# Column tiles on x without scales in the opening of a hybrid attention layer

## The chip, the cores and the metric

The kernel runs on one core of a Trainium2 chip. The metric is the device time of one execution in microseconds (us). Engines: PE is TensorE (matrix products; PEld its weight loads), DVE is VectorE, ACT is ScalarE, POOL is GpSimd, and SP is the engine whose queue issues all loads and stores of this kernel. Each engine runs its instructions in the order in which they stand in its queue; one that waits holds up all behind it.

## The reference

One decoder layer over 2048 tokens with 1024 features, with 16 meta tokens ahead of them. What matters here is the head of it:

```python
def rms_norm(x, g):
    xf = x.astype(jnp.float32)
    y = xf * lax.rsqrt(jnp.mean(xf * xf, axis=-1, keepdims=True) + RMS_EPS)
    return (y * g.astype(jnp.float32)).astype(x.dtype)
...
    h = jnp.concatenate([pad, meta, x], axis=1)
...
        xn = rms_norm(h, norm_gain[l])
        proj = xn @ w_in[l]
        sb_q, sb_k, sb_v, sw_q, sw_k, sw_v, sb_z, sw_z, g_sb, g_sw = jnp.split(proj, offsets, axis=-1)
```

The columns of `proj` are the queries, keys and values of a stick-breaking attention (sb), those of a sliding-window attention (sw), and four gates. Both attentions, the gated branch projections, the output projection with the residual and a final norm follow. Each row of x has one scale (the rsqrt of its mean square) and each feature one gain, so `xn @ w` is also (x times gain) `@ w`, multiplied by the scale of its row afterwards.

## The kernel before

Tokens are cut into four groups of 512 (`GT`), features into eight blocks of 128 (`KT`). A **column tile** is 128 columns of `proj` for one group: its result stands transposed in one PSUM bank, columns on partitions and tokens along the bank. All products are made at nearly full precision from two parts: x and the weights are each split into a high part (rounded) and a low part (the difference), `xh`, `xl`, `wh`, `wl`. A column tile is then 8 blocks x 3 products = 24 products of 128x512 (`gemm`, L357 to L359). The tiles that also need the meta tokens append 16 small products to bank `zm` (L365).

The first two groups to run are 2 and 3 (`halves`). For each group the program

- loads x in rows, eight pieces of 128x512, squares them on ACT with a sum per row (L313), and works out the scale of each row (`scales`, `rsqrt`; L314, L117 to L124);
- spreads the scales over a bank with four transposes on TensorE (`spread`, L323) and copies them to `rb` (L335);
- loads x transposed (`xt`) in eight blocks, multiplies each by gain and `rb` on DVE (L341), casts to `xh` on ACT (L342) and takes `xl` on DVE, or on POOL for two blocks of the first group (L343).

A weight tile (`weights`) is a load of 512 KB (`raw`), a cast to `wh` (ACT at L106 in the opening, POOL at L108 later) and a difference `wl` (L109, on POOL in the opening, on DVE after it). Both halves are written to DRAM, for the second half of the program reads them again.

TensorE's instructions run in the order of the program text (`tc.manual_schedule`). For the other engines and for SP's queue a planner chooses the order. The opening is: scales of group 2 and of the meta tokens; `prep` of group 2; sb_k0 and sb_q0 on group 2, their products interleaved; scales and `prep` of group 3; sb_k1 on group 2; the same three tiles on group 3; then sw_k on both groups, sw_v on both groups, and the queries. What a tile does with its bank stands in its `use`: for sb_k and sb_q a high and a low part (L112, L113) written to DRAM; for sw_k the rotary embedding (L545 to L549) and four copies (L557, L559). Meta columns of sb_k are turned by a small transpose later (`meta_cols`, L377), in a function put on `pending`, which runs inside the next tile after its seventh block (`lagged`).

PSUM banks are rings by name: g and z and t have two, zm and o have one.

Of the kernel before, what the change touches and what calls it, by code (L numbers as in the profile page):

```python
# [16 lines left out]
P = 128  # L17
D = 1024
# [21 lines left out]
def f32(ap):  # L40
    return ap.bitcast(F32)
# [3 lines left out]
def tile_kernel(ctx, tc, x, xt, meta, metat, gain, w_in, w_sb, w_sw, w_out, sinks, fgain,  # L45
# [106 lines left out]
    wp = ctx.enter_context(tc.tile_pool(name="w", bufs=1, side="right"))  # L152

    kept = {}

    def weights(c0, w=w_in):
# [8 lines left out]
        raw = wp.tile([P, KT, P], F32, tag="raw", name="raw", bufs=2)[:, :n, :]  # L165
        DMA(raw, w[c0 // P])
        split(wh, wl, raw)
        kept[key] = [dram(f"{t}_{w.name}_{c0}", [P, n, P], F32R) for t in "hl"]
        for t, k in zip((wh, wl), kept[key]):
            DMA(k, t)  # L170
        return wh, wl


# [129 lines left out]
    def ring_x(dt=F32):  # L303
        return tp.tile([P, GT], dt, tag="xs", name="xs", bufs=XS)

    def scales(src, rows, n, mk=ring_x):

        ssq = tp.tile([P, 2, 4], F32, tag="ssq", name="ssq", bufs=2)
        for i in range(n):
            for f in range(2):  # L310
                t = mk()
                DMA(t[:rows], src[i * rows:(i + 1) * rows, f * GT:(f + 1) * GT])
                A.activation(t[:rows], t[:rows], AF.Square, accum_out=ssq[:rows, f, i:i + 1])  # L313
        V.tensor_tensor(ssq[:rows, 0, :n], ssq[:rows, 0, :n], ssq[:rows, 1, :n], op=ALU.add)  # L314
        rs = tp.tile([P, 4], F32, tag="rs", name="rs", bufs=2)
        rsqrt(rs[:rows, :n], ssq[:rows, 0, :n], tp)
        return rs
# [5 lines left out]
            T.transpose(acc[:, i * rows:(i + 1) * rows], rs[:rows, i:i + 1].to_broadcast([rows, P]), ident[:rows, :rows])  # L323
        return acc[:, :n * rows]

    def group_scales(g, mk=ring_x):
        return scales(x[g * GT:(g + 1) * GT, :], P, 4, mk)

    def prep(g, rs, mk=ring_x, pool=False, mid=lambda: None):

        xh[g] = xp.tile([P, KT, GT], F32R, tag=f"xh{g % 2}", name="xh")
        xl[g] = xp.tile([P, KT, GT], F32R, tag=f"xl{g % 2}", name="xl")
        rows = spread(rs, P, 4)
        rb = tp.tile([P, GT], F32, tag="rb", name="rb", bufs=1)
        A.copy(rb, rows)  # L335
        for k in range(KT):
            if k == MID:
                mid()
            t = mk()
            DMA(t, xt[g, k])  # L340
            V.scalar_tensor_tensor(t, t, gn[:, k:k + 1], rb, op0=ALU.mult, op1=ALU.mult)  # L341
            A.copy(xh[g][:, k, :], t)  # L342
            (G if pool and k in XP else V).tensor_tensor(xl[g][:, k, :], t, f32(xh[g][:, k, :]), op=ALU.subtract)  # L343

    def prep_meta(rs):
        t = ring_x()[:, :KT * NM].rearrange("p (k t) -> p k t", k=KT)
# [7 lines left out]
    def gemm(acc, w, g, pm=None):  # L354
        wh, wl = w
        for k in range(KT):
            T.matmul(acc, lhsT=wh[:, k, :], rhs=xh[g][:, k, :], start=k == 0, stop=False)  # L357
            T.matmul(acc, lhsT=wh[:, k, :], rhs=xl[g][:, k, :], start=False, stop=False)  # L358
            T.matmul(acc, lhsT=wl[:, k, :], rhs=xh[g][:, k, :], start=False, stop=k == KT - 1)  # L359
            if k < KT - 1 or pm is not None:  # L360
                yield 0.65
        if pm is not None:
            for k in range(KT):
                for t in (wh, wl):
                    T.matmul(pm[:48, :P], lhsT=mx[:, k, :], rhs=t[:, k, :], start=k == 0 and t is wh,  # L365
                             stop=k == KT - 1 and t is wl)

    def meta_sum(pm):

        t = tmp(rows=NM)[:, :P]  # L370
        A.copy(t, pm[32:48, :P])
        V.tensor_tensor(t, pm[0:NM, :P], t, op=ALU.add)
        return t

    def meta_cols(ms):
        tr = ps("zm")
        T.transpose(tr[:, :NM], ms, ident[:NM, :NM])  # L377
        return tr[:, :NM]

# [475 lines left out]
    hsplit[0] = False  # L855
    rs = group_scales(halves[0][1])
    for half, groups in enumerate(halves):
        with tc.tile_pool(name=f"swa{half}", bufs=1, side="left") as sp:
            m = half == 0
            vsplit[0] = True  # L860
            if not m:
                ts = [mk() for mk in sbt[:3]]
                rs = rs1
            if m:
                for _ in zip(*(by_group([t], groups[:1], m) for t in ts[:2])):
                    pass
                flush_all()
            else:
                drain(by_group(ts[:2], groups[:1], m))
            prep(groups[1], rs)  # L870
            drain(by_group(ts[2:], groups[:1], m), by_group(ts, groups[1:]))
# [12 lines left out]
            flush_all()  # L884
        with tc.tile_pool(name=f"sb{half}", bufs=1, side="left") as bp:
            vsplit[0] = False
            side = stick(groups, bp)
            drain(tiles_by_tile(gts[2:3], groups))
            if half == 0:
                rs0, rs1 = (group_scales(g) for g in halves[1])  # L890
            n_mid = 22 if half == 0 else 20
            cost_sb = 8 * sum(4 * (4 - g) for g in groups) * 1.31 + 16 * 0.75
            weave(tiles_by_tile(gts[3:3 + n_mid], groups), side, cost_sb / (n_mid * 10.4))
            drain(side)
        if half == 0:
            ts = [mk() for mk in gts[3 + n_mid:]]
            drain(by_group(ts, groups[:1]), by_group(ts[:1], groups[1:]))
            prep(halves[1][0], rs0)
            drain(by_group(ts[1:], groups[1:]))
        else:  # L900
            ringl = rings()
            osw = {}
            todo = [(k, g) for k in range(8) for g in halves[0]]
            for mk in gts[3 + n_mid:]:
                if mk is gts[-1]:
                    with tc.manual_schedule(engines={mybir.EngineType.Activation}):
                        drain(tiles_by_tile([mk], groups))
                        A.preload_act_table_set("natural_log_exp_and_others")
# [58 lines left out]
```

## Time and profile before

| | us |
|---|---|
| median of 3 runs | 2213.93 |
| lowest and highest | 2213.37, 2215.7 |
| profiled execution | 2219.62 |
| its span | 2217.9 |

The profile shows one execution. Its page gives for each engine the busy time, its share of the span and the number of instructions. The timeline has one row for each instruction or run of like ones: start and duration in us, engine, line, operation, output <- inputs, shape, and in brackets the idle time before it and what ended it. The view of windows has for each stretch its length, the busy time of PE, PEld, DVE, ACT and POOL with instruction counts, TensorE's granted clock, the DMA share and GB/s. TensorE's granted clock over the whole execution is 0.993 of full speed.

### The profile page before, as it was taken

Reading aid. Unit: us, or ns where it says so; the run is one execution under the profiler, and the core shown is the slowest. Engines: PE = TensorE matmul, PEld = TensorE weight load, DVE = VectorE, ACT = ScalarE, POOL = GpSimd, SP = SyncE. Lnnn points to the kernel's source line nnn. Section 1 sums busy time; section 2 is a strip of 40 time slices with the busy share of each in tenths; the row PEclk is TensorE's granted clock in tenths of the full one; section 3 lists DMA queues with packets and bytes.
Section 4 is the critical chain, followed back from the end, with each engine's and each line's share of the span. In section 5 each row is a group of like instructions: output and inputs, shape, how many; then the busy total and the mean of one; then the engine's idle time right before and its main releaser. Section 6 shows DMA issues by size and latency. Waiting matters only on the chain.

```text
span 2217.9 us, 30245 instructions
## 1 busy us (share of the span) xinstructions
PE 2158.9 (97%) x10614; PEld 1773.3 (80%) x10614; DVE 1352.5 (61%) x2105; ACT 1004.6 (45%) x2325; POOL 384.8 (17%) x495
## 2 busy tenths in 40 slices
PE   4999999999999999999999999999999999999998
PEld 3878887788888887788887888888888888787886
DVE  4568776455554433677666888777774436454453
ACT  5457777433333323577764555555553301221121
POOL 2123333323223201133220000000000232000000
PEclk9999999999999999999999999999999999999999
DMA  8645456855555465444436433324323986368522
GB/s 295 216 159 180 172 172 225 274 183 190 173 168 177 144 212 185 161 171 159 154 132 186 119 118 111 117 93 131 115 84 108 350 287 199 137 221 281 164 89 86
DMA packets 175385, 382.48 MB, mean 172 GB/s; under 512 B 22945, under 2 KB 41057, under 8 KB 175233
## 3 DMA queue, kind: packets, MB, share of 16 engines
q1 hardware_dynamic: 175232, 380.54, 50.9%
q8 instruction: 84, 1.38, 0.3%
q14 instruction: 69, 0.56, 0.1%
HBM read 231.04 MB, written 149.36 MB: 172 GB/s over the span
## 4 chain that ended last, share of the span: by engine, by line
PE 91%; DMA 3%; DVE 2%; issue 2%; ACT 1%; POOL 0%; SPq 0%; DVEq 0%; POOLq 0%; ACTq 0%
PE ps_g L357 16%; PE ps_g L358 15%; PE ps_g L359 15%; PE ps_o L808 6%; PE ps_z L760 6%; PE ps_t L782 5%; PE ps_o L669 3%; PE ps_z L623 3%; PE ps_g L212 1%; PE ps_g L213 1%; PE ps_g L211 1%; PE ps_z L212 1%; PE ps_z L211 1%; PE ps_z L213 1%; PE ps_t L212 1%
## 5 line engine op out<-in xcount | busy, mean ns | idle before, releaser
L357 PE MATMUL ps_g<-xh,wh 128*128 128x512 f32 x1600 | 663.5, 415 | 4.2 <-ACT xh L342 2.2
L358 PE MATMUL ps_g<-xl,wh 128*128 128x512 f32 x1600 | 632.5, 395 | 6.2 <-DVE xl L343 6.2
L359 PE MATMUL ps_g<-xh,wl 128*128 128x512 f32 x1600 | 632.2, 395 | 0.0
L771 DVE TENSOR_TENSOR_SCAN row<-row 128x512 f32<-128x512 f32 (+2 forms) x320 | 367.8, 1152 | 198.7 <-POOL row L769 122.4
L359 PEld LDWEIGHTS ps_g<-xh,wl 128*128 128x128 f32 x1600 | 303.0, 189 | 68.0
L357 PEld LDWEIGHTS ps_g<-xh,wh 128*128 128x128 f32 x1600 | 304.4, 190 | 54.2 <-DVE tmp L547 2.8
L358 PEld LDWEIGHTS ps_g<-xl,wh 128*128 128x128 f32 x1600 | 304.4, 190 | 52.3 <-DVE xl L343 7.3
L764 ACT ACTIVATE row<-ps_z 128x512 f32<-128x512 f32 (+1 forms) x320 | 172.1, 538 | 285.1 <-PE ps_z L760 236.5
L113 DVE SCALAR_TENSOR_TENSOR wtl<-ps_t,wth 128x512 fp32r<-128x512 f32 (+1 forms) x320 | 190.4, 595 | 45.8 <-ACT wth L112 44.3
L112 ACT ACTIVATE wth<-ps_t 128x512 fp32r<-128x512 f32 (+1 forms) x320 | 170.4, 532 | 101.1 <-PE ps_t L782 96.3
L760 PE MATMUL ps_z<-kt,q 128*128 128x512 f32 (+3 forms) x640 | 185.1, 369 | 0.3 <-ACT row L764 0.3
L782 PE MATMUL ps_t<-ident,row 128*128 128x128 f32 x1088 | 171.6, 273 | 1.2 <-DVE row L771 1.2
L782 PEld LDWEIGHTS ps_t<-ident,row 128*128 128x128 f32 x1088 | 136.0, 140 | 37.8 <-DVE row L771 1.7
L769 POOL TENSOR_SCALAR_AFFINE_SELECT row<-row 128x128 f32<-128x128 f32 x128 | 42.8, 335 | 621.4 <-ACT row L764 563.6
L108 POOL TENSOR_SCALAR wh<-raw 128x1024 fp32r<-128x1024 f32 (+1 forms) x71 | 74.2, 1045 | 426.0 <-PE ps_g L358 267.7
L760 PEld LDWEIGHTS ps_z<-kt,q 128*128 128x128 f32 x640 | 118.9, 188 | 26.4 <-ACT row L764 0.8
L808 PE MATMUL ps_o<-wth,vc 128*128 128x512 f32 (+1 forms) x320 | 125.1, 391 | 0.2
L631 ACT ACTIVATE sc<-sc,nm 128x129 f32<-128x129 f32 x256 | 100.1, 394 | 38.0 <-DVE nm L629 37.4
L808 PE MATMUL ps_o<-wtl,vc 128*128 128x512 f32 (+1 forms) x320 | 116.8, 365 | 0.0
L499 ACT ACTIVATE tmp<-ps_g 128x512 f32<-128x512 f32 x112 | 67.1, 599 | 100.7 <-PE ps_g L359 94.2
L109 POOL TENSOR_TENSOR wl<-raw,wh 128x1024 fp32r<-128x1024 f32 (+1 forms) x45 | 102.9, 2287 | 18.7 <-ACT wh L106 15.6
L250 ACT CAST ringl<-gt 128x512 fp32r<-128x512 f32 x32 | 19.9, 622 | 127.0 <-DVE gt L248 120.3
(222 smaller groups left out, 3337.2 us busy)
## 6 DMA issues: line engine op xcount, KB each, us to landing
raw<-in_w_in SPq DMA_DIRECT2D x58, 512.0 KB, 5.1
h_in_w_in<-wh SPq DMA_DIRECT2D x58, 512.0 KB, 3.1
l_in_w_in<-wl SPq DMA_DIRECT2D x58, 512.0 KB, 3.1
wh<-h_in_w_in SPq DMA_DIRECT2D x58, 512.0 KB, 3.7
wl<-l_in_w_in SPq DMA_DIRECT2D x58, 512.0 KB, 4.8
q<-qd SPq DMA_DIRECT2D x128, 128.0 KB, 3.9
vc<-vd SPq DMA_DIRECT2D x48, 256.0 KB, 2.9
qd<-tmp SPq DMA_DIRECT2D x32, 256.0 KB, 2.4
```

The lines of the kernel that those rows point to most:

```text
L109: (V if vsplit[0] else G).tensor_tensor(l, src, f32(h), op=ALU.subtract)
L112: A.activation(h, acc, AF.Copy, scale=scale)
L113: V.scalar_tensor_tensor(l, acc, scale, f32(h), op0=ALU.mult, op1=ALU.subtract)
L357: T.matmul(acc, lhsT=wh[:, k, :], rhs=xh[g][:, k, :], start=k == 0, stop=False)
L358: T.matmul(acc, lhsT=wh[:, k, :], rhs=xl[g][:, k, :], start=False, stop=False)
L359: T.matmul(acc, lhsT=wl[:, k, :], rhs=xh[g][:, k, :], start=False, stop=k == KT - 1)
L631: A.activation(sc[:, hh, :], sc[:, hh, :], AF.Exp, bias=nm[:, hh:hh + 1], accum_out=den[:, hh:hh + 1])
L760: T.matmul(z[:, :w], lhsT=lq, rhs=kt[h][:, k0:k0 + w], start=t == 0, stop=t == 1)
L764: A.activation(r[:, :w], z[:, :w], AF.Sigmoid, scale=-1.0)
L771: V.tensor_tensor_scan(r[:, :w], r[:, :w], r[:, :w], last[j] if n else 1.0, op0=ALU.mult, op1=ALU.min)
L782: T.transpose(tr[:, j * P:(j + 1) * P], rows_of[h, g, n - (j > i), j][:, k0:k0 + P], ident)
L808: T.matmul(o[:, :n], lhsT=v, rhs=r, start=first and r is wh, stop=last and r is wl)
```

## The change

The opening (the "start" pool and what follows up to the windows) is written anew, with DVE, ACT and SP in the order of the program text too.

- The three tiles sb_k0, sb_q0 and sb_k1 of groups 2 and 3 run on x times gain without scales (`unscaled`: high part on ACT, low part on DVE, no `rb`). Their six banks (g, g, z; z, o, t) are multiplied by `rb` afterwards (`out_of`), and the result goes to the tile's `use`.
- The normalised x of both groups, which sw_k and all later tiles use, is made afterwards: for group 2 in place from the blocks loaded at first (`raws`), for group 3 from a second load of its blocks.
- x for the scales comes as whole blocks of 128x1024 (`wide`; one of group 2's four as two halves) and is squared ahead of use.
- Meta products are separated from the tiles (`gemm_meta`, `meta_product`).
- The first three weight tiles take `wl` on DVE (`vsplit`), and the stores of weight halves are put off (`put_off`). The weights of sw_k and sw_v are loaded in the opening (`raw2`, `ready`).
- Pairs or threes of `normal` go in turns (`in_turns`), so that DVE and ACT alternate between blocks.
- sw_k and sw_v then run by group: both on 2, then both on 3. The meta columns of sb_k1 go to a t bank instead of zm.

```diff
+    put_off, ready = [], {}
...
+    def weights(c0, w=w_in, raw=None):
+
+        if c0 in ready:
+            return ready.pop(c0)
...
-            DMA(k, t)
+            if put_off is None:
+                DMA(k, t)
+            else:
+                put_off.append((k, t))
...
+    def normal(g, k, t, rb):
+        V.scalar_tensor_tensor(t, t, gn[:, k:k + 1], rb, op0=ALU.mult, op1=ALU.mult)
+        A.copy(xh[g][:, k, :], t)
+        yield
+        V.tensor_tensor(xl[g][:, k, :], t, f32(xh[g][:, k, :]), op=ALU.subtract)
...
-                    mc = meta_cols(ms)
+                    mc = meta_cols(ms, "zm" if p != 1 else "t")
...
-    with tc.tile_pool(name="start", bufs=1, side="left") as bp:
-        mk = lambda: bp.tile([P, GT], F32, tag="x0", name="x0", bufs=17)
-        rs = group_scales(halves[0][0], mk)
-        rsm = scales(meta, NM, 1)
-        ts = [sbt[0]()]
-        prep(halves[0][0], rs, mk, True, lambda: ts.append(sbt[2]()))
-    prep_meta(rsm)
-    hsplit[0] = HS
-    ts.append(sbt[1]())
-    hsplit[0] = False
-    rs = group_scales(halves[0][1])
+    g0, g1 = halves[0]
+    with (tc.tile_pool(name="start", bufs=1, side="left") as bp,
+          tc.manual_schedule(engines={mybir.EngineType.DVE, mybir.EngineType.Activation, mybir.EngineType.SP})):
+        hsplit[0] = vsplit[0] = True
...
+        def unscaled(g, k, t):
+
+            DMA(t, xt[g, k])
+            uh, ul = xh["u", g][:, k, :], xl["u", g][:, k, :]
+            A.activation(uh, t, AF.Copy, scale=gn[:, k:k + 1])
+            V.scalar_tensor_tensor(ul, t, gn[:, k:k + 1], f32(uh), op0=ALU.mult, op1=ALU.subtract)
...
+        def out_of(g, n, rb):
+            t = tmp()
+            V.tensor_tensor(t, accs[g, n], rb, op=ALU.mult)
+            yield
+            ts[n][1](g, t, ms[n] if g == g0 else None)
...
+        ts = [sbt[0]()]
+        x_tiles(("u", g0), 1)
+        for k in range(KT):
+            raws.append(bp.tile([P, GT], F32, tag="raw0", name="raw0", bufs=KT))
+            unscaled(g0, k, raws[k])
+        ts.extend([sbt[2](), sbt[1]()])
+        rsm = scales(squares(meta, NM, 1), NM, 1)
+        products(g0, 0, "g")
+        products(g0, 1, "g")
+        prep_meta(rsm)
...
+        rows = [wide(g0, i) for i in range(3)]
+        for i, t in enumerate(rows):
+            square(t, ssq0, i)
...
+        rs = scales(ssq0, P, 4)
+        products(g0, 2, "z")
...
+        for k in range(KT):
+            if k == 2:
+                rb0 = scale_rows(rs, bp.tile([P, GT], F32, tag="rb0", name="rb0"))
+            unscaled(g1, k, bp.tile([P, GT], F32, tag="raw1", name="raw1", bufs=4))
+        products(g1, 0, "z")
+        x_tiles(g0, 0)
+        rows = [wide(g1, i) for i in range(3)]
+        raw2 = [load(c) for c in (C_SWK, C_SWV)]
...
+        for k in range(0, KT, 2):
+            in_turns(*(normal(g0, j, raws[j], rb0) for j in (k, k + 1)))
+            if k == 2:
+                meta_product(0)
+            if k:
+                square(rows[k // 2 - 1], ssq1, k // 2 - 1)
+        t = wide(g1, 3)
...
+        square(t, ssq1, 3)
+        products(g1, 1, "o")
+        meta_product(2)
+        hsplit[0] = False
+        ready.update({c: weights(c, raw=raw) for c, raw in zip((C_SWK, C_SWV), raw2)})
+        new = [ring_x() for _ in range(4)]
+        for k, t in enumerate(new):
+            DMA(t, xt[g1, k])
+        in_turns(*(out_of(g0, n, rb0) for n in range(2)))
+        rs = scales(ssq1, P, 4)
+        products(g1, 2, "t")
+        rb1 = scale_rows(rs)
+        for k, t in put_off:
+            DMA(k, t)
+        x_tiles(g1, 1)
+        in_turns(out_of(g0, 2, rb0), normal(g1, 0, new[0], rb1))
+        for k in range(1, KT):
+            if k >= 4:
+                new.append(ring_x())
+                DMA(new[k], xt[g1, k])
+        in_turns(*(normal(g1, j, new[j], rb1) for j in (1, 2)))
+        in_turns(*(normal(g1, j, new[j], rb1) for j in (3, 4)))
+        in_turns(*(normal(g1, j, new[j], rb1) for j in (5, 6, 7)))
+    put_off = None
+    for n in range(3):
+        drain(out_of(g1, n, rb1))
...
-            drain(tiles_by_tile([sw_k, sw_v], groups, m), tiles_by_tile(q[0], groups[:1]), tiles_by_tile(sbt[3:4], groups, m))
+            if m:
+                drain(by_group([sw_k(), sw_v()], groups, m))
+            else:
+                drain(tiles_by_tile([sw_k, sw_v], groups))
+            drain(tiles_by_tile(q[0], groups[:1]), tiles_by_tile(sbt[3:4], groups, m))
```

More of the change, by code (lines that the diff above doesn't have):

```diff
@@ L154, in tile_kernel, with load @@
     kept = {}
-    def weights(c0, w=w_in):
+    put_off, ready = [], {}
+    def load(c0, w=w_in):
+        raw = wp.tile([P, KT, P], F32, tag="raw", name="raw", bufs=2)[:, :w.shape[2], :]
+        DMA(raw, w[c0 // P])
+        return raw
+    def weights(c0, w=w_in, raw=None):
+        if c0 in ready:
+            return ready.pop(c0)
         n = w.shape[2]
@@ L164, in weights @@
             return wh, wl
-        raw = wp.tile([P, KT, P], F32, tag="raw", name="raw", bufs=2)[:, :n, :]
-        DMA(raw, w[c0 // P])
+        raw = load(c0, w) if raw is None else raw
         split(wh, wl, raw)
@@ L324, in spread, with group_scales, scale_rows, x_tiles @@
         return acc[:, :n * rows]
[L326 to L335, printed above, removed]
+    def group_scales(g):
+        return scales(squares(x[g * GT:(g + 1) * GT, :], P, 4), P, 4)
+    def scale_rows(rs, rb=None):
+        if rb is None:
+            rb = tp.tile([P, GT], F32, tag="rb", name="rb", bufs=1)
+        A.copy(rb, spread(rs, P, 4))
+        return rb
+    def x_tiles(key, n):
+        xh[key] = xp.tile([P, KT, GT], F32R, tag=f"xh{n}", name="xh")
+        xl[key] = xp.tile([P, KT, GT], F32R, tag=f"xl{n}", name="xl")
+    def normal(g, k, t, rb):
[3 more added lines that the diff above has]
+        V.tensor_tensor(xl[g][:, k, :], t, f32(xh[g][:, k, :]), op=ALU.subtract)
+    def prep(g, rs):
+        x_tiles(g, g % 2)
+        rb = scale_rows(rs)
         for k in range(KT):
-            if k == MID:
-                mid()
-            t = mk()
+            t = ring_x()
             DMA(t, xt[g, k])
-            V.scalar_tensor_tensor(t, t, gn[:, k:k + 1], rb, op0=ALU.mult, op1=ALU.mult)
-            A.copy(xh[g][:, k, :], t)
-            (G if pool and k in XP else V).tensor_tensor(xl[g][:, k, :], t, f32(xh[g][:, k, :]), op=ALU.subtract)
+            drain(normal(g, k, t, rb))
     def prep_meta(rs):
@@ L362, in gemm, with gemm_meta @@
         if pm is not None:
[L363 to L366, printed above, removed]
+            gemm_meta(pm, w)
+    def gemm_meta(pm, w):
+        for k in range(KT):
+            for t in w:
+                T.matmul(pm[:48, :P], lhsT=mx[:, k, :], rhs=t[:, k, :], start=k == 0 and t is w[0],
+                         stop=k == KT - 1 and t is w[1])
     def meta_sum(pm):
-        t = tmp(rows=NM)[:, :P]
+        t = tp.tile([NM, P], F32, tag="ms", name="ms", bufs=2)
         A.copy(t, pm[32:48, :P])
@@ L863, in tile_kernel @@
                 rs = rs1
[L864 to L871, printed above, removed]
+            if not m:
+                drain(by_group(ts[:2], groups[:1]))
+                prep(groups[1], rs)
+                drain(by_group(ts[2:], groups[:1]), by_group(ts, groups[1:]))
             if m:
```

48 lines of the change are left out of this document (43 added, 5 removed).

## Prediction

> **What bounds the kernel now.** I read the page first, then TensorE's waits in the first 160 us, then the timeline there.
>
> ```profile
> span 2217.9 us, 30245 instructions
> PE 2158.9 (97%) x10614; PEld 1773.3 (80%) x10614; DVE 1352.5 (61%) x2105; ACT 1004.6 (45%) x2325; POOL 384.8 (17%) x495
> ...
> PE ps_t L323 <- DVE nwt L123: 17.8, 1, 17.8
> PE ps_t L323 <- DVE rs L124: 5.8, 1, 5.8
> PE ps_g L358 <- DVE xl L343: 3.9, 1, 3.9
> ```
>
> TensorE is busy for 97% of the span, and most of what is left is in the opening: 17.8 us until the scales of the first group (2) exist, 3.9 for its first low part, 5.8 for the scales of group 3 (target, releaser, us in total, times, longest). Everything behind the opening moves with it, so the question is at what time TensorE has the column tiles of the opening behind it.
>
> ```profile
> 21.04 0.79 PE L357 MATMUL ps_g<-xh,wh 128*128 128x512 f32 x1 [1.93 <-ACT xh L342]
> 25.71 0.79 PE L358 MATMUL ps_g<-xl,wh 128*128 128x512 f32 x1 [3.87 <-DVE xl L343]
> ...
> 39.18 0.22 PE L365 MATMUL ps_zm<-wh,mx 128*48 128x128 f32 x1
> ...
> 46.99 1.11 PE L323 MATMUL ps_t<-ident,rs 128*128 128x128 f32 x4 [5.80 <-DVE rs L124]
> 47.75 0.78 PE L357 MATMUL ps_g<-xh,wh 128*128 128x512 f32 x1
> 48.33 0.63 PE L358 MATMUL ps_g<-xl,wh 128*128 128x512 f32 x1
> 48.75 0.63 PE L359 MATMUL ps_g<-xh,wl 128*128 128x512 f32 x1
> ...
> 55.41 0.96 PE ps_zm L365 x16
> ...
> 72.80 0.39 PE L359 MATMUL ps_g<-xh,wl 128*128 128x512 f32 x1
> 73.02 0.39 PE L357 MATMUL ps_g<-xh,wh 128*128 128x512 f32 x1
> ...
> 97.98 0.59 ACT L416 COPY tmp<-ps_g 128x512 f32<-128x512 f32 x1 [0.16 <-PE ps_g L359]
> ```
>
> Starts 0.22 to 0.23 us apart are TensorE's full pace (72.80, 73.02), 0.43 its pace after a long wait (48.33, 48.75). A column tile of 24 products is thus 5.46 us. Six tiles (sb_k0, sb_q0, sb_k1 for two groups) come first, then sw_k and sw_v. The first product of sw_k stands at 73.02, and the last of sw_v at 97.9, where ACT reads its bank. These are my two marks. Work ahead of 73.0 is only 6 x 5.46 + 2 meta products at 0.96 (row x16, from the chain of waits): 35 us, so 38 us are lost.
>
> **The change part by part.** I carry the clock forward by the rows.
>
> *Tiles of group 2 without scales.* x-transposed and weights are loaded first; only gain is multiplied in, so the scales leave the front of the path.
>
> ```profile
> 1.70 3.90 SPq L55 DMA_DIRECT2D x<-in_x  x8
> 4.75 0.63 ACT L313 ACTIVATE x<-x 128x512 f32<-128x512 f32 x1 [2.69 <-DMA x<-in_x]
> 8.63 0.63 ACT L313 ACTIVATE x<-x 128x512 f32<-128x512 f32 x1 [0.51 <-DMA x<-in_x]
> 5.00:10.00 5.00, 0.00 (x0) 0.00 (x0) 0.00 (x0) 3.29 (x10) 0.00 (x0) 1.00 0.94 333
> 10.00:15.00 5.00, 0.00 (x0) 0.00 (x0) 0.79 (x5) 4.71 (x16) 0.22 (x1) 1.00 1.02 368
> 20.00:25.00 5.00, 0.79 (x1) 0.29 (x1) 5.00 (x6) 2.80 (x5) 2.63 (x1) 1.00 1.05 407
> 13.67 1.03 ACT L106 CAST wh<-raw 128x1024 fp32r<-128x1024 f32 x1
> 14.78 2.34 POOL L109 TENSOR_TENSOR wl<-raw,wh 128x1024 fp32r<-128x1024 f32 x1 [11.74 <-ACT wh L106]
> 14.83 2.30 DVE L121 TENSOR_TENSOR nwt<-rs 128x4 f32<-128x4 f32 x1 [0.81 <-ACT rs L119]
> 63.54 1.22 DVE L109 TENSOR_TENSOR wl<-raw,wh 128x1024 fp32r<-128x1024 f32 x1
> ```
>
> SP needs 0.49 us for an issue (3.90 for 8), so weights and eight blocks are issued by 6.1; the x loads for the squares, whole blocks now, are queued behind them. The first load of 256 KB landed at 4.75, the fourth at 8.63; later ones follow at 333 to 368 GB/s, at most 407 (last number of the window rows). The first weight block (512 KB) lands near 6, its cast takes 1.03 and its low part, now on DVE, 1.22 instead of 2.34 on POOL: ready at 8.2, with the first block of x (7.4 + two operations of about 0.65 = 8.7). Product 24 needs the eighth block, about 2.7 MB into the stream: 13 us. Some 11 products run at 0.43 until 13.5, 13 at 0.23: tile one ends at 16.2, tile two (sb_q0) at **21.7**. Before, tiles one and two, interleaved, ended at 39.2 (first meta product of L365).
>
> *Squares behind the meta tokens.* ACT's hand-made order has the copy of mx, which waits for a transpose behind tile two, ahead of the squares of x. So these begin at 22.7: three of 128x1024, at 1.03 for such a cast plus the read-out, about 1.2 each, and two of 128x512 at 0.8: 27.9. Group 2's scales then take what the chain below took.
>
> ```profile
> 45.24 0.16 DVE L314 TENSOR_TENSOR ssq<-ssq 128x4 f32<-128x4 f32 x1 [3.22 <-ACT xs L313]
> 48.14 0.59 ACT L335 COPY rb<-ps_t 128x512 f32<-128x512 f32 x1 [2.00 <-PE ps_t L323]
> 48.76 2.08 DVE L341 SCALAR_TENSOR_TENSOR xs<-xs,gn,rb 128x512 f32<-128x512 f32 x3 [1.83 <-ACT rb L335]
> 52.02 1.89 DVE L343 TENSOR_TENSOR xl<-xs,xh 128x512 fp32r<-128x512 f32 x3
> raw<-in_w_in SPq DMA_DIRECT2D x5, 512.0 KB, 5.9
> kd<-tmp SPq DMA_DIRECT2D x4, 256.0 KB, 2.0
> ```
>
> From L314 at 45.24 to the transposes at 46.99 is 1.75 us: 29.7. TensorE has meanwhile ended tile three at 27.5.
>
> *Group 3 without scales.* It has four buffers for eight blocks: loads five to eight each wait on SP until DVE is done with a block. Their landing is bounded by 2.0 (kd, empty queue) and 5.9 (raw, full queue); I take 2.5, since nothing else is in flight there. DVE starts at 29.7 and loses 1.2 to the copy of rb0, which ACT can do only after the transposes; so blocks three and four leave their buffers at 32.6 and 33.2, the last load lands at 35.7 and its two operations end at 36.9 (36.4 and 40.3 by the bounds). TensorE ends tile four at **37.6**; the last three products are all that is left then. Tiles five and six and two meta products (2 x 5.46 + 2 x 0.96) follow without a new wait: **50.4**.
>
> *DVE is the engine that is late next.* The edit gives it 16 unscaled low parts (0.65 each), 6 products with rb (0.66), 3 weight splits (1.22): 18 us more, and prep's 16 pairs stay. From 36.9: eight pairs of group 2 at 0.69 + 0.63 (rows x3: 2.08 and 1.89 by three) are 10.5, to 47.5; the sum of the second meta product waits for ACT's last square, 49.6; two weight splits 2.4; two products and two low parts 2.5; group 3's scales 1.75: 56.3. One thing adds to this: the high halves of the sw_k and sw_v weights stay on POOL and fall beside these DVE operations.
>
> ```profile
> 85.40 1.05 POOL L108 TENSOR_SCALAR wh<-raw 128x1024 fp32r<-128x1024 f32 x1 [0.47 <-POOL tmp L549]
> 85.47 1.00 DVE L548 TENSOR_TENSOR tmp<-tmp,sm 128x16 f32<-128x16 f32 x1
> ```
>
> A DVE operation on 16 columns took 1.00 beside such a POOL split, as the one on 4 took 2.30 above. The two splits cost DVE 0 to 2.1; I take 1, because DVE waits for ACT there anyway: **57.2**. The Trainium skill (SBUF — State Buffer, "SBUF: two separate sides") says that DVE and GpSimd lock one port pair for a whole instruction when the DVE operation has two SBUF inputs. These two rows agree with it (1.00 beside 1.05); by that rule all 2.1 would be paid and the sum below would be 1 us longer.
>
> *The mark.* The scale transposes of group 3 stand in TensorE's order ahead of sw_k. TensorE waits from 50.4 to 57.2 and starts sw_k at 58.0 (46.99 to 47.75 in the rows), against 73.0: 15.0 earlier. After so long a wait ten products run at 0.43 again: 2.1 back, so 12.9.
>
> *What is left to wait for.* From 57.2 DVE has the rest of its hand-made order: one product and its low part, eight pairs for group 3 (10.5), with about 2 of waits for ACT and for the last four loads behind four ring buffers: until 71.7. Behind it come three products with rb1, which release banks z, o and t, and the two small L399 parts. TensorE, in sw_k's first tile after its seventh block (64.6), transposes the two meta columns, the second into a t bank that the third product frees; and sw_k's own meta product goes into zm, which L399 reads. If DVE fits these four small operations into its gaps, TensorE runs on until sw_k of group 3 (73) needs x that is ready at 72 to 74. The low bound of these waits is 0, the high one 11.6 (second rival); I take 3.5, because DVE has two such gaps, and because of this:
>
> ```profile
> L187 ACT CAST ringl<-tmp x16: 620/622/629, 1718.1 to 1759.7; 128x512 fp32r<-128x512 f32 x16
> L908 ACT ACT_TABLE_LOAD  x1: 1283/1283/1283, 1755.5 to 1755.5; - x1
> ```
>
> L908 is in a hand-ordered part of ACT; casts of L187, outside it and emitted before it, ran until 1759.7. So operations outside a hand-ordered part do mix with it.
>
> *At no cost:* 2.1 MB of group 3 read twice and ten kept weight halves written later. They lie under TensorE's 13 us of tiles five and six and DVE's chain; without that cover the second reading costs 5 us at 407 GB/s. Of SP's issues in the two groups 32 loads of x become 33.
>
> **Sum:** 15.0 - 2.1 - 3.5 = 9.4 us, taken as 9 of the profiled span of 2217.9 (2219.6 with what lies around it). That execution stands 5.7 above the median of 2213.9; from the median, **2205**.
>
> **Rivals.**
>
> *Nothing waits behind the mark:* 12.9 us, **2201**. For it: x of group 3 is ready block by block. Against: DVE is the busiest engine there.
>
> *The banks are held to the end of DVE's order.* Then TensorE stands from 65.5 until the third product at 73.6, again from 74.4 to 75.9 for L399, and runs slow once more: 11.6 us. Gain 1.3: **2213**. For it: program order. Against: the L187 rows. This is also the case in which the change does not do what it says, TensorE being no earlier.
>
> *Slower: loads behind few buffers.* If the two sets of four loads land as in a full queue (5.9 less 2.5, of which 0.5 hides: 2.9 each), DVE's order ends at 77.5 instead of 71.7, and with the banks held 5.8 - 1.3 = 4.5 us are lost: **2218**. It decides from 73.0 on for the end of DVE's order. For it: writes of the kept weights are queued ahead of the second set. Against: those 2 MB have 6 us to drain.
>
> **How the numbers follow.** The forecast has 0.52, the first rival 0.16, the second 0.16, the third 0.16. A measurement here tells 0.2% (4.4 us) from no change. Faster by more: the first two cases, 0.68; within: 0.16; slower: 0.16. The forecast's own range is 2201 to 2209 (0 to 8 us of left waits); for 8 in 10 I go down to 2199, as the marks are good to 2 us, and up to 2217, short of the last rival.
>
> **What would show it.** TensorE's first product near 8 and not 21; the wait for group 3's scales near 50 to 57 as its longest; sw_k's first product at 58 (55 to 61); DVE without gaps from 30 to 57 but for the waits named; in sw_k's first tile no wait over 4 us on a bank read by DVE; ACT's read of the last sw_v bank at 88 or 89 instead of 97.9. Wrong would be a sw_k start after 66, or a wait of 8 us behind it.

## The result, and the profile after

| | before | after |
|---|---|---|
| median (9 runs each), us | 2215.58 | 2221.02 |
| lowest and highest | 2213.37, 2217.69 | 2216.67, 2224.83 |
| profiled execution, its span | 2219.62, 2217.9 | 2224.83, 2223.1 |
| ratio after to before, 95% interval | | 1.0028 [1.0019, 1.0037] |

The change makes the kernel 0.28% slower: 5.4 us more, where 2205 (10.6 less than this median of before) was forecast, with a range that ended at 2217. In the changed kernel `gemm` is L382 to L384, the meta products L393, the meta transposes L405, the copies of meta columns L426 (ACT) and L427 (DVE), `spread` L339, the rope L573 to L577, `out_of` L907. TensorE's waits of the first 160 us (target, releaser, us in total, times, longest):

```profile
PE ps_zm L393 <- DVE tmp L427: 11.2, 1, 11.2
PE ps_t L339 <- DVE rs L124: 7.9, 2, 6.3
PE ps_g L382 <- ACT xh L884: 7.4, 1, 7.4
PE ps_zm L393 <- DVE tmp L575: 3.3, 1, 3.3
```

The long waits of before (17.8 and 3.9 for group 2) are gone. Two new ones stand on bank zm, both at a meta product. The timeline of TensorE has the start of sw_k and both waits:

```profile
57.96 1.11 PE L339 MATMUL ps_t<-ident,rs 128*128 128x128 f32 x4 [6.31 <-DVE rs L124]
58.72 0.77 PE L382 MATMUL ps_g<-xh,wh 128*128 128x512 f32 x1
...
65.82 0.23 PE L405 MATMUL ps_zm<-ident,ms 16*128 16x16 f32 x1
...
78.25 0.34 PE L393 MATMUL ps_zm<-wh,mx 128*48 128x128 f32 x1 [11.24 <-DVE tmp L427]
...
91.19 0.34 PE L393 MATMUL ps_zm<-wh,mx 128*48 128x128 f32 x1 [3.35 <-DVE tmp L575]
```

sw_k starts at 58.72 instead of 73.02, **14.3 us earlier**. What follows takes it all back. The prediction's second mark was ACT's read of the last sw_v bank: 97.98 before, 88 or 89 forecast, 107.43 measured. ACT comes to that bank late in the changed kernel, behind four copies for sw_k, so the next bank is the better end of sw_k and sw_v: ACT's first read of a bank of the queries, in the timelines of before and of after.

```profile
103.92 0.59 ACT L545 ACTIVATE tmp<-ps_g 32x512 f32<-32x512 f32 x1 [0.16 <-PE ps_g L359]
```

```profile
104.87 2.54 ACT L585 CAST kk<-tmp 64x512 fp32r<-64x512 f32 x4 [2.78 <-POOL tmp L577]
107.43 0.59 ACT L444 COPY tmp<-ps_g 128x512 f32<-128x512 f32 x1
...
111.05 0.59 ACT L573 ACTIVATE tmp<-ps_g 32x512 f32<-32x512 f32 x1
```

This first read of a query bank is called **the mark** from here on. From the start of sw_k to it, it is 52.3 us after and 30.9 before, 21.4 more: 14.6 in the two waits (11.24 + 3.35), and the other 6.8 at a lower pace. The windows say where (length, then busy time and instructions of PE, PEld, DVE, ACT, POOL, then TensorE's granted clock, DMA share, GB/s), first before, then after:

```profile
58.00:80.00 22.00, 22.00 (x110) 18.00 (x109) 8.53 (x14) 3.22 (x8) 3.16 (x3) 1.00 0.81 288
80.00:100.00 20.00, 20.00 (x102) 16.35 (x101) 14.42 (x24) 13.33 (x29) 5.22 (x5) 1.00 0.38 127
100.00:2300.00 2200.00, 2088.96 (x10285) 1716.72 (x10283) 1300.13 (x2014) 958.47 (x2220) 362.26 (x470) 0.99 0.48 162
```

```profile
25.00:35.00 10.00, 7.82 (x32) 4.73 (x30) 5.24 (x12) 7.51 (x16) 0.00 (x0) 1.00 0.40 117
35.00:52.00 17.00, 15.76 (x88) 11.88 (x86) 14.27 (x21) 10.30 (x19) 2.10 (x2) 1.00 1.00 352
52.00:58.00 6.00, 0.04 (x1) 0.05 (x1) 5.20 (x13) 1.64 (x4) 0.00 (x0) 0.87 1.01 388
58.00:80.00 22.00, 10.76 (x47) 8.56 (x47) 14.76 (x24) 6.95 (x13) 3.14 (x5) 0.66 1.04 396
80.00:100.00 20.00, 16.66 (x74) 13.33 (x73) 9.92 (x22) 9.89 (x25) 2.38 (x3) 0.82 0.09 26
100.00:2300.00 2200.00, 2095.03 (x10317) 1721.34 (x10315) 1308.22 (x2022) 963.31 (x2229) 366.23 (x473) 1.00 0.48 163
```

Between 58 and 80 TensorE does 47 instructions where it did 110, at a clock of 0.66. Behind 100 us 10317 are left against 10285: 32 more, at 5.46/24 us each 7.3, which is the 7.1 by which the mark is later. The span grew by 5.2. The DMA engines are full from 35 to 80 after they had stood at 0.40 from 25 to 35.

What TensorE waits for 11 us is a copy of 128x16. The timelines of ACT and DVE show how it comes to be so late:

```profile
61.98 0.62 ACT L112 ACTIVATE tmp<-tmp 128x512 fp32r<-128x512 f32 x1
...
69.02 0.63 ACT L112 ACTIVATE tmp<-tmp 128x512 fp32r<-128x512 f32 x1 [0.65 <-DVE tmp L907]
75.38 0.63 ACT L112 ACTIVATE tmp<-tmp 128x512 fp32r<-128x512 f32 x1 [5.74 <-DMA kd<-tmp]
76.82 0.17 ACT L426 CAST tmp<-ps_zm 128x16 fp32r<-128x16 f32 x1 [0.80 <-DVE tmp L113]
```

```profile
76.05 0.69 DVE L113 SCALAR_TENSOR_TENSOR tmp<-tmp 128x512 fp32r<-128x512 f32 x1 [4.95 <-ACT tmp L112]
...
78.02 0.17 DVE L427 TENSOR_TENSOR tmp<-ps_zm,tmp 128x16 fp32r<-128x16 f32 x1
```

The meta transpose filled zm at 65.8 (L405 above). Its copy L426 stands in ACT's queue behind the high parts (L112) of group 3's three tiles. The last of these needs a free `tmp` tile, of which there are seven. By the order of the program one of them held the product that this step reads, and the other six held parts whose stores had not landed. ACT stands for 5.74 us; behind it come the low part L113 on DVE, L426, L427, and then TensorE. In the stretch 52 to 80 the stores took this long (queue's issues: count, KB each, median us to landing):

```profile
kd<-tmp SPq DMA_DIRECT2D x8, 256.0 KB, 6.6
h_in_w_in<-wh SPq DMA_DIRECT2D x3, 512.0 KB, 6.1
```

Before, four such stores of `kd` took 2.0 up to 60 us (their row stands in the prediction), and four more took 4.8 between 60 and 75. So the chain has four links: full DMA engines, seven `tmp` tiles, the place of the small copies in the queues, and one bank zm for both the transposes and the meta products. The experiments cut these links, alone and together.

A fifth link stands in SP's queue, and no run here cut it alone. The store that ACT waited for is, by the order of the program, the first of these two:

```profile
67.88 1.95 SPq L55 DMA_DIRECT2D kd<-tmp  x2
```

Its part was written by 62.6 (L112 at 61.98), and the low part that is stored with it by 63.3. SP issued the store only at 67.88, behind stores of weights and the loads of `ct` and `sn`, and it then took 7.4 us to land. So some 5 of its 12.8 us passed in SP's queue.

### The profile page after: what moved, and what is told of

It reads as the page before. It is cut to its first block, busy times and chain, and to the rows that moved or that the text cites. A ratio compares the mean times of both kernels' runs of the same rounds, so it can differ in the third digit from the quotient of the medians.

```text
span 2223.1 us, 30264 instructions
## 1 busy us (share of the span) xinstructions
PE 2163.1 (97%) x10614; PEld 1773.3 (80%) x10614; DVE 1369.6 (62%) x2134; ACT 1013.7 (46%) x2327; POOL 376.3 (17%) x490
## 5 line engine op out<-in xcount | busy, mean ns | idle before, releaser
L382 PE MATMUL ps_g<-xh,wh 128*128 128x512 f32 x1568 | 650.8, 415 | 9.7 <-ACT xh L884 7.4
L383 PE MATMUL ps_g<-xl,wh 128*128 128x512 f32 x1568 | 619.9, 395 | 3.6 <-DVE xl L359 3.0
L384 PE MATMUL ps_g<-xh,wl 128*128 128x512 f32 x1568 | 619.1, 395 | 0.0
L384 PEld LDWEIGHTS ps_g<-xh,wl 128*128 128x128 f32 x1568 | 296.8, 189 | 66.5
L382 PEld LDWEIGHTS ps_g<-xh,wh 128*128 128x128 f32 x1568 | 298.4, 190 | 58.4 <-ACT xh L884 7.4
L383 PEld LDWEIGHTS ps_g<-xl,wh 128*128 128x128 f32 x1568 | 298.4, 190 | 48.8 <-DVE xl L359 4.0
L113 DVE SCALAR_TENSOR_TENSOR wtl<-ps_t,wth 128x512 fp32r<-128x512 f32 (+1 forms) x320 | 190.3, 595 | 45.0 <-ACT wth L112 43.5
L112 ACT ACTIVATE wth<-ps_t 128x512 fp32r<-128x512 f32 (+1 forms) x320 | 170.4, 532 | 101.0 <-PE ps_t L810 96.3
L109 POOL TENSOR_TENSOR wl<-raw,wh 128x1024 fp32r<-128x1024 f32 (+1 forms) x42 | 94.8, 2257 | 3.2
```

Of the source, the lines that this page charges most:

```text
L109: (V if vsplit[0] else G).tensor_tensor(l, src, f32(h), op=ALU.subtract)
L112: A.activation(h, acc, AF.Copy, scale=scale)
L113: V.scalar_tensor_tensor(l, acc, scale, f32(h), op0=ALU.mult, op1=ALU.subtract)
```

## The experiments

All start from the changed kernel; line numbers behind an edit shift by up to four. "Left" is the number of TensorE instructions behind 100 us in the profiled execution; "mark" is the mark above. Both are of one execution each: group 3's scales came at 57.96 in the changed kernel and at 59.33 and 59.15 in e2 and e3, which are alike up to there, so marks are good to some 1.5 us. Theory T blames the full DMA engines and late stores, theory Z the bank zm and the order by hand, whatever the bytes; in the later runs O is the place in the queues and the order of DVE's and ACT's work, S the slots and stores.

| run | edit | median (runs) | ratio to before, 95% | mark | left |
|---|---|---|---|---|---|
| changed kernel | | 2221.02 (9) | 1.0028 [1.0019, 1.0037] | 111.05 | 10317 |
| e1 | kept weight halves stored earlier | 2221.09 (9) | 1.0023 [1.0013, 1.0033] | 112.70 | 10326 |
| e4 | four blocks of x not loaded twice | 2222.79 (7) | 1.0026 [1.0015, 1.0036] | 110.19 | 10313 |
| e2 | three more tiles | 2214.02 (11) | 0.9996 [0.9987, 1.0005] | 103.80 | 10285 |
| e3 | meta products in bank z | 2214.19 (12) | 0.9995 [0.9986, 1.0005] | 103.46 | 10283 |
| m5 | small copies placed by hand | 2215.70 (12) | 1.0001 [0.9993, 1.0009] | 105.18 | 10291 |
| m6 | e3, e4 and m5 | 2214.06 (11) | 0.9992 [0.9983, 1.0001] | 102.13 | 10278 |
| m7 | no order by hand | 2218.02 (10) | 1.0009 [0.9999, 1.0018] | 106.77 | 10298 |
| m8 | two low parts back on POOL | 2220.21 (10) | 1.0019 [1.0010, 1.0029] | 109.21 | 10309 |
| n9 | e3, sw_v first | 2215.42 (11) | 1.0002 [0.9994, 1.0011] | 105.50 | 10280 |
| n10 | m6, sw_v first | **2208.29** (8) | **0.9969 [0.9958, 0.9980]** | 100.81 | 10260 |
| n11 | n10 and three more tiles | 2210.75 (12) | 0.9986 [0.9977, 0.9994] | 101.87 | 10261 |
| n12 | n10 without e4 | 2213.47 (12) | 0.9991 [0.9980, 1.0003] | 105.14 | 10279 |

### Less traffic: e1 and e4

```diff
+            if k == 4:
+                for d, w in put_off:
+                    DMA(d, w)
+                del put_off[:]
             if k == 2:
```

e1 issues the six put-off stores in the middle of the loop over group 3's unscaled blocks, where the DMA engines had room.

> Mark M: ACT's first read of the first query bank, 103.92 in the kernel before, 111.05 in the changed one. Theory T (the 16 DMA engines are full from 34 to 82 us, stores of kd land late, the ring of tmp stays occupied, ACT stands 5.7 us and TensorE 11.2 us behind it): the six put-off stores (3.1 MB, 7.9 us at 400 GB/s) now run from 18 to 29 us, where nothing was moved; ACT's wait of 5.7 goes, TensorE's wait on zm falls from 11.2 to 3 to 6, M at 104 to 106, time 5 to 7 us below the changed kernel. Rival Z (TensorE waits on zm because of the order by hand, whatever the bytes): the wait stays at 10 to 12 and M at 110 to 112.

2221.09. ACT's wait for a store falls to 3.5 us and the wait on zm to 8.6, but that for group 3's scales grows from 6.3 to 9.0 (they come at 61.88 instead of 57.96), and the second one on zm to 4.0. The traffic moved and the time did not; as the edit also held up the scales, this run alone does not decide on theory T.

e4 keeps the last four raw blocks of group 3 and multiplies them again in place, so that four loads of 256 KB go:

```diff
-            unscaled(g1, k, bp.tile([P, GT], F32, tag="raw1", name="raw1", bufs=4))
+            late.append(bp.tile([P, GT], F32, tag="raw1", name="raw1", bufs=4))
+            unscaled(g1, k, late[k])
...
-        for k in range(1, KT):
-            if k >= 4:
-                new.append(ring_x())
-                DMA(new[k], xt[g1, k])
+        new += late[4:]
```

> Blocks 4 to 7 of group 3 are kept from the first reading (their four buffers are the last used), so four loads of 1 MB and their waits for ring buffers are gone. T: 2.6 us less of queue, the last low part of group 3 at 70 to 74 instead of 87.5, wait on zm 7 to 9, M at 107 to 109, time 2 to 4 us below the changed kernel. Z: the wait on zm stays within 1 us of 11.2, M at 110 to 112.

2222.79, no gain. Its ACT has no wait for a store any more up to the small copy, and TensorE still waits 10.4 us on zm. DVE's timeline in e4:

```profile
60.21 1.23 DVE L109 TENSOR_TENSOR wl<-raw,wh 128x1024 fp32r<-128x1024 f32 x1 [0.65 <-DMA kd<-tmp]
...
63.32 0.69 DVE L113 SCALAR_TENSOR_TENSOR tmp<-tmp 128x512 fp32r<-128x512 f32 x1 [1.21 <-ACT tmp L112]
...
77.30 0.63 DVE L113 SCALAR_TENSOR_TENSOR tmp<-tmp 128x512 fp32r<-128x512 f32 x1
77.85 0.16 DVE L427 TENSOR_TENSOR tmp<-ps_zm,tmp 128x16 fp32r<-128x16 f32 x1
```

From 63.9 to 78 no row has a wait of over 0.2. The x of the last four blocks is there early, so all of it is done ahead of the small copy, which runs at 77.85 against 78.02. The late store and the full queue of DVE each are enough to make TensorE wait until 78: with the one gone, the other stands there. Theory T alone falls.

### Slots and bank: e2 and e3

```diff
+        def out_of(g, n, rb, mk=tmp):
+            t = mk()
...
-    for n in range(3):
-        drain(out_of(g1, n, rb1))
+    with tc.tile_pool(name="mid", bufs=1, side="left") as mp:
+        for n in range(3):
+            drain(out_of(g1, n, rb1, lambda: mp.tile([P, GT], F32, tag="mid", name="mid", bufs=3)))
```

> Only the products with rb1 of group 3 get three tiles of their own, so that tmp has three more slots. If the occupied ring is the link between the full DMA engines and TensorE: ACT's wait of 5.7 on a kd store goes, the wait on zm falls from 11.2 to 5 to 6, M at 105 to 106, time 5 us below the changed kernel. If the late loads of group 3 are the link: the wait on zm moves by less than 2 us, M at 109 to 111.

2214.02: 7 us better than the changed kernel. With tiles of their own the three products with `rb1` come at 62.4 to 64.2 on DVE, ACT waits 3.0 us for a store, right ahead of the small copy, where it had waited 5.7, L427 runs at 74.28, and TensorE's waits in this stretch are

```profile
PE ps_zm L393 <- DVE tmp L427: 7.0, 1, 7.0
PE ps_zm L393 <- DVE tmp L575: 1.4, 1, 1.4
```

e3 leaves slots and queues alone and gives the meta products of sw_k and sw_v a z bank:

```diff
-        pm = ps("zm") if first else None
+        pm = ps(pmb[0]) if first else None
...
+                pmb[0] = "z"
                 drain(by_group([sw_k(), sw_v()], groups, m))
+                pmb[0] = "zm"
```

> The meta products of sw_k and sw_v go to the two z banks, free by then, instead of the one zm bank. Bytes and loads stay. Rival Z: both waits on zm (11.2 and 3.3) go, TensorE goes on to sw_k of group 3, whose last block of x is there at 87.5, M at 99 to 101, time 8 to 11 us below the changed kernel. Theory T in its strong form (DMA sets the pace of everything there): the waits move to x of group 3 or to bank g, M not below 108.

2214.19. ACT still waits 5.2 for a store, but TensorE need not wait with it until later:

```profile
PE ps_zm L405 <- DVE tmp L429: 5.2, 1, 5.2
PE ps_g L382 <- DVE tmp L577: 2.1, 1, 2.1
```

So a cut at either link brings 7 us, about what the change lost, and neither brings what it was to gain.

### Place in the queues: m5, m6, m7, m8

m5 runs the pending small copies by hand right behind the first of group 3's steps, into tiles of their own:

```diff
         in_turns(out_of(g0, 2, rb0), normal(g1, 0, new[0], rb1))
+        auto, small[0] = small[0], lambda: bp.tile([P, NM], F32R, tag="mc", name="mc", bufs=4)
+        flush(pending)
+        small[0] = auto
```

> The copies and low parts of sb_k's meta columns (L426, L427), which stood behind the six steps of out_of of group 3 on ACT and DVE, are put into the order by hand right behind the third tile of group 2, with small tiles of their own. Bytes, loads and all other work stay. Theory O (their place in the queues is what TensorE waits for): the wait on zm in sw_k falls from 11.2 to under 1, TensorE goes on to sw_v of group 2 until 73, and waits there for sw_k's evacuation or for the last block of x of group 3; M (first read of the first query bank, 111.05 in the changed kernel, 103.92 before) at 102 to 105, time 6 to 9 us below the changed kernel. Theory S (late stores and occupied slots set the pace of all that follows): ACT's wait of 5.7 stays, TensorE's wait moves to the next tile at nearly full length, M not below 108.

2215.70. The low parts now run at 63.80 and 64.48, and the wait of sw_k's meta product is gone, as theory O said. A wait comes back one tile later, at sw_v's, as theory S said:

```profile
PE ps_zm L393 <- DVE tmp L577: 9.3, 1, 9.3
```

L577 is the rope of sw_k's own meta columns (L575 before the edit). It stands behind group 3's normal x, a wait of DVE of 2.05 us for a store of `kd`, and one of 1.27 for the load of the sine table. The edit does more than move the copies: TensorE's two small transposes come ahead of sw_k with them (59.64 and 60.39), and the copies leave the ring of `tmp`. So it does not part place from slots cleanly. m6 joins e3, e4 and m5.

> The meta copies by hand, the meta products in z, and blocks 4 to 7 of group 3 kept. O with DVE as the limit: DVE has no gap from 58 to about 76, then evacuates sw_k of group 2; sw_k of group 3 starts at 77 to 80, M at 95 to 99, time 12 to 16 us below the changed kernel and 6 to 10 below the kernel before (ratio 0.995 to 0.997). S: M not below 102, ratio 0.998 or more.

2214.06. Theory O had expected a mark of 95 to 99 and 12 to 16 us below the changed kernel; the mark is 102.13 and it is 7 us, which is what theory S allowed. One wait is left behind sw_k's start: 6.3 us for a g bank, held by the rope of sw_k's first group (L579), which is late in DVE's queue and waits 1.8 us there for the cosine table.

m7 takes away the order by hand for DVE, ACT and SP.

```diff
-    with (tc.tile_pool(name="start", bufs=1, side="left") as bp,
-          tc.manual_schedule(engines={mybir.EngineType.DVE, mybir.EngineType.Activation, mybir.EngineType.SP})):
+    with tc.tile_pool(name="start", bufs=1, side="left") as bp:
```

> The same program without the order by hand on DVE, ACT and SP: the planner orders them. If the order by hand is the cause of the loss, M falls to 108 or less. If it is what brings sw_k forward to 58.7, the planner puts group 2's normalisation ahead of group 3's unscaled parts on DVE, sw_k starts at 62 or later and M is 113 or more, time 2 us or more above the changed kernel.

2218.02, 3 us better than the changed kernel. Both expectations came true in part: the scales of group 3 come later (62.13), and the mark is at 106.77 all the same. TensorE waits 8.6 on group 3's unscaled blocks at 41.5 and still 10.8 on zm, for the planner's order puts the small copies no earlier (L427 at 79.18). But it does not wait for the scales then, and the second wait on zm is 0.5 instead of 3.3. So the order by hand costs some 3 us, and not by the place of the small copies; which part of it does was not tested, for everything moves at once here. m8 takes the low parts of the sw_k and sw_v weights on POOL instead of DVE (`vsplit[0] = False` around their `weights`).

> Only the low parts of the sw_k and sw_v weights go back to POOL (2.3 us each there). DVE is free of 2.47 us at 51: the scales of group 3 and sw_k's start come 2 to 2.5 us earlier (56.3). If DVE's amount of work sets the end of the wait on zm, L427 comes 2 us earlier (76) and M is 108.5 to 109.5; if stores and slots set it, L427 stays at 78 and M within 0.7 of 111.

2220.21, which the intervals do not tell from the changed kernel. The scales of group 3 come only 0.3 us earlier (spread at 57.64), so DVE's two weight splits are not what they wait for. Behind them more moves: L427 runs at 75.23 and the mark is 1.8 earlier, as was expected if DVE's amount of work sets the end of the wait on zm.

```profile
75.23 0.17 DVE L427 TENSOR_TENSOR tmp<-ps_zm,tmp 128x16 fp32r<-128x16 f32 x1
```

But ACT's wait for a store is shorter there as well (1.7 instead of 5.7), so the run does not part the two.

### sw_v first: n9 to n12

sw_v's bank is read by one copy on ACT, sw_k's by the rope on both engines. With sw_v first, the g bank that TensorE needs two tiles later comes free without DVE.

```diff
-                drain(by_group([sw_k(), sw_v()], groups, m))
+                drain(by_group([sw_v(), sw_k()], groups, m))
```

(The loads and splits of the two weights change places as well, and the store of `kk` moves to sw_k.)

> The meta products of sw_k and sw_v go to a z bank, as in the earlier run with that edit alone (2214 us, ACT's first read of a query bank at 103.5), and sw_v runs ahead of sw_k in both groups, so that the first g bank of the two is read out by one copy on ACT and not by the rotary embedding on DVE. If DVE's queue is what TensorE waits for (theory O), the wait of 2.1 on a g bank held by the rotary embedding goes, and that for the small transpose of 5.2 stays: mark near 101, about 2212. If the part behind the mark takes up what the opening gives (rival A), the mark falls and the time stays at 2214 to 2216.

2215.42: e3's wait of 2.1 on the g bank falls to 0.2, but a new one of 8.6 stands on sw_v's transposes, whose copy is behind ACT's wait for a store. With sw_v first alone nothing is won. The mark was expected near 101 and is 105.5. n10 is m6 with sw_v first:

> As the run with meta products in z, meta copies by hand and four blocks kept (2214 us, mark 102.1, one wait of 6.3 on the g bank of sw_k), with sw_v ahead of sw_k. By theory O the 6.3 goes, since TensorE's next g bank is read out by ACT alone, some 3 us earlier, and the rotary embedding has a whole column tile more: mark 97 to 99, about 2208 to 2210. By the theory of full slots and late stores (S) the rotary embedding's own tiles are still held by late stores, and a wait of 4 us or more stays: mark 101 to 102, 2213. By rival A the mark falls below 99 and the time stays at 2213 to 2216.

2208.29, 0.9969 [0.9958, 0.9980]: **faster than both kernels**. The waits from 40 to 115 us and the windows:

```profile
PE ps_t L339 <- DVE rs L124: 6.2, 1, 6.2
PE ps_zm L452 <- ACT tmp L448: 3.2, 1, 3.2
PE ps_t L405 <- ACT rb L348: 0.5, 1, 0.5
```

```profile
58.00:80.00 22.00, 17.41 (x86) 13.88 (x86) 18.54 (x35) 10.17 (x21) 1.60 (x5) 0.81 0.90 337
100.00:2300.00 2200.00, 2081.40 (x10260) 1711.19 (x10258) 1299.93 (x2015) 957.07 (x2221) 362.93 (x470) 1.00 0.48 162
```

The 6.3 on the g bank is gone as theory O said, 3.2 on ACT's copy stands in its place. DVE is busy for 18.5 of 22 us from 58 to 80, where it was 14.8 in the changed kernel, and 25 TensorE instructions fewer are left behind 100 us than before the change: 5.7 us of the 6.5 measured. The mark, expected at 97 to 99, is 100.8; with sw_k last it stands behind the rope on ACT and does not compare to the others.

> The run before with three tiles more for the products with the scales. By O no more than 1 us is gained on it, as DVE is in step with its own work there: mark 97 to 99. By S 3 us or more: what is left of the waits goes with the slots, mark near 95, 2207.

2210.75: three more tiles on top give nothing, as theory O said, so slots are not short any more.

> The run with sw_v first, meta products in z and meta copies by hand (2208.29 us), but with all eight blocks of group 3 loaded a second time: 1 MB more in the time in which the DMA engines are full. By theory O (the order in which DVE and ACT do their work) the blocks come ahead of their turn on DVE anyway: 2208 to 2210, and no more than 10 TensorE instructions more are left behind 100 us than the 10260 of that run. By theory S (full slots, late stores, full DMA engines) the loads come late again and DVE with them: 2212 to 2214, and some 20 instructions more.

2213.47, 19 instructions more than n10: here theory S was right and O wrong. With all eight blocks loaded again one long wait of TensorE is left, on x (and one of 1.0 on zm):

```profile
PE ps_g L383 <- DVE xl L359: 7.2, 1, 7.2
```

DVE's timeline of n12 has the last block behind the rope, and the rope behind a load:

```profile
82.16 0.69 DVE L579 SCALAR_TENSOR_TENSOR tmp<-ps_g,ct 128x512 f32<-128x512 f32 x1 [2.17 <-DMA ct<-in_cost]
84.22 0.69 DVE L580 TENSOR_TENSOR tmp<-tmp,sn 128x512 f32<-128x512 f32 x1 [1.37 <-DMA sn<-in_sint]
84.94 0.75 DVE L356 SCALAR_TENSOR_TENSOR xs<-xs,gn,rb 128x512 f32<-128x512 f32 x1
85.61 2.96 DVE L359 TENSOR_TENSOR xl<-xs,xh 128x512 fp32r<-128x512 f32 x3
```

So the second loads, worth nothing as long as the small copies were late (e4), cost about 5 us (0.9991 against 0.9969; the two intervals just touch) once these are in place. Order and traffic had hidden each other.

## Why the prediction was wrong

**The front: right.** First product at 7.42 (8 forecast); group 3's scales at 57.96 and sw_k at 58.72 (57.2 and 58.0). Of 15.0 us 14.3 came. "At no cost" held this far: neither the second reading nor the late stores delayed sw_k. For the two POOL splits 1 us of 0 to 2.1 was taken. Two rows of DVE in the changed kernel, the second beside a split at 45.18, put it at 0.87 (2.23 against 1.36); the other split, at 50.45, fell for the most part into a wait of DVE's:

```profile
41.65 1.36 DVE L359 TENSOR_TENSOR xl<-raw,xh 128x512 fp32r<-128x512 f32 x2
...
44.55 2.23 DVE L359 TENSOR_TENSOR xl<-raw,xh 128x512 fp32r<-128x512 f32 x2
```

The Trainium skill's rule (SBUF — State Buffer, "SBUF: two separate sides") agrees with the row that met a split. The prediction's use of that rule would have charged both splits, whether DVE was at work beside them or not.

**The slow clock: right in kind, too small.** 2.1 us was booked for one restart. There were three, as each new wait brought another: 78.25 to 83.9 and 91.19 to 94.2 ran at half pace too. Together they cost 6.8.

**The failing step** is "If DVE fits these four small operations into its gaps, TensorE runs on", from which 3.5 us of left waits was taken. The changed kernel has 14.6 there. The upper bound of 11.6 held a restart of 2.1 as well; with the restarts behind the waits (6.8 - 2.1) it is 19.3 against it. A wait of 8 us behind sw_k's start was the prediction's own sign of being wrong, and the first was 11.2. Three things in the step did not hold:

- It looked at DVE's gaps alone. L427 needs L426 first, and ACT's queue stood behind a tile that a store still held (e2: 3.0 of the 5.7 us left, L427 at 74.28 instead of 78.02, 7 us better).
- The rows of L187 were read as if an operation that mixes with a hand-made order also goes first. Operations did mix (the weight split L109 of the queries ran on DVE at 59.53, ahead of group 3's first block), but the small copies were placed behind the six steps of `out_of`, and by the planner's own order no earlier (m7).
- DVE's order was to end at 71.7, with the three products behind it. In n10, where ACT waits for no store, it still ends at 78.2 (rows of L359; DVE itself waits 1.5 at 61): from 58 on the products with `rb1`, their low parts and a weight split are done among x's blocks.

**At no cost: wrong behind the mark.** The 13 us of tiles five and six and DVE's chain did not drain the traffic: the DMA share was 1.0 from 35 to 80, and stores took 6.6 instead of 2.0. That the engines would stand at 0.40 from 25 to 35, and so push their work behind, was not foreseen. The 2.0 that the prediction calls the landing time in an empty queue is right for its four stores up to 60 us; it was not the time behind the mark even before the change, where four took 4.8.

Two of the prediction's sums are a little off, by less than 1 us each: 13 products at 0.23 from 13.5 on end at 16.5 rather than 16.2, and 57.2 with 1.3, 10.5 and 2 gives 71 rather than 71.7 for the end of DVE's order.

**The rivals.** The second (banks held to the end of DVE's order, chance 0.16) named the bank, the engine and the slow restart; its 2213 came from an end at 73.6, and the end was 78. The third had the slower side from late transfers and an end of 77.5, 2218, which is near the time; but there it was late loads, and here it was late stores, so that it came near is chance. It takes the two together to lose more than the front won: 14.3 - 14.6 - 6.8 = -7.1 at the mark, where the prediction had 15.0 - 3.5 - 2.1 = 9.4. Why the span lost only 5.2 of it was not followed.

## What to carry to other kernels

When a stage is pulled forward, its small consumers must come forward in the queues as well: follow each bank that the next stage needs through every engine's queue that releases it, down to the store that frees its tile and the queue that issues this store. Price "transfers lie under other work" by the landing time in a full queue, not by bytes. Where two causes hold the same instruction to the same time, taking away one shows nothing; try them together before calling either harmless.

## What the hardware showed that was not expected

An issue by SP itself took longer in a run of issues while the DMA engines were full. SP's queue in the changed kernel, at a DMA share of 1.04:

```profile
61.40 1.18 SPq L55 DMA_DIRECT2D ct<-in_cost  x1
62.63 1.18 SPq L55 DMA_DIRECT2D sn<-in_sint  x1
...
65.92 0.33 SPq L55 DMA_DIRECT2D h_in_w_in<-wh  x1
```

1.18 us in the run, against 0.33 for the same 512 KB after a pause. In n10, where the DMA share from 77 to 84 us is 0.68, SP issued the same `ct` and `sn` in 0.33 and 0.43; what sets it was not tested.

And a wait of 3.17 us was enough for half pace: in n10 the meta products behind it start 0.107 us apart (78.83, 78.93, 79.04), where 0.06 is full pace. In e4 even 2.12 us were enough, and the pace fell only behind the wait: its first meta products start 0.06 apart, from 90.86 on they are 0.1 apart, and the products of the next block 0.43.

```profile
89.98 0.26 PE L393 MATMUL ps_zm<-wh,mx 128*48 128x128 f32 x1 [2.12 <-DVE tmp L575]
...
91.59 0.63 PE L383 MATMUL ps_g<-xl,wh 128*128 128x512 f32 x1
92.01 0.63 PE L384 MATMUL ps_g<-xh,wl 128*128 128x512 f32 x1
```

The Trainium skill (TensorE: Matmul & The Clock Gate, "Part 1: The HAM clock gate (the "warmup" mystery)") has the clock fall after an idle window of about 3.4 us; both of these waits are shorter, and here the measurement decides.
